# Conditioning vectors moved wholly to VectorE, a quarter of each weight's low part to GpSimd, coarse recurrence copies to ScalarE

## The chip, the cores and the metric

The kernel runs on one core of one Trainium2 chip. The metric is device time in microseconds (us) of one execution, the median of several; lower is better. The engines are named as in the profile: PE is TensorE (matmuls; PEld its weight loads), DVE is VectorE, ACT is ScalarE, POOL is GpSimd, and SP is the queue that issues the loads.

## The reference

Two layers of a decoder trunk on 256 tokens of 1024 channels in float32. A conditioning vector `c` scales, shifts and gates each layer; four token mixers run beside each other; an MLP with 4096 hidden channels follows.

```python
    for l in range(DEPTH):
        cmod = (c_act @ ada_w[l] + ada_b[l])[:, None, :]
        sh1, sc1, g1, sh2, sc2, g2 = jnp.split(cmod, 6, axis=-1)
        h = _rmsnorm(x, norm_mix_g[l]) * (1.0 + sc1) + sh1
        z = h @ w_in[l]
        ...
        ya = _conv_branch(za, conv_w[l], conv_b[l], conv_ln_g[l], conv_ln_b[l])
        yb = _sparse_attn_branch(zb, positions)
        yc = _gla_branch(zc, gla_gate_w[l], gla_gate_b[l], gla_norm_g[l])
        yd = _hgrn2_branch(zd, lower_bounds[l], hgrn_norm_g[l])
        ...
        x = x + g1 * (merged @ w_o[l])
        h = _rmsnorm(x, norm_mlp_g[l]) * (1.0 + sc2) + sh2
        x = x + g2 * (jnp.square(jax.nn.relu(h @ mlp_w1[l])) @ mlp_w2[l])
```

The six parts of `cmod` (1024 numbers each) are numbered 0 to 5 in the order of the split, so that (1, 2) is the gate `g1` of layer 1. Branches C and D are gated linear recurrences.

## The kernel before

All weights pass once through one stream of slabs of 128 x 1024 float32 (512 KB), in the order in which TensorE uses them. A slab is loaded by an SP-issued DMA into one of five `raw` places. `do_split` (L429) then makes two parts of it: ScalarE rounds it to `wh` in float32r, and VectorE subtracts, `wl = raw - wh`. TensorE multiplies three times per tile: high by high, high by low, low by high. The `raw` place is free, and the next load can start, when `wl` is there. `wh` and `wl` have five places, with four more in part of the program.

The order of instructions on each engine is fixed when the program is built: the class `Flow` (L96) emits the stream and weaves in chains of smaller work (attention, recurrences, convolution, norms) by a rough model of the engines' clocks, whose costs stand in `_Meter` (L222). On the chip each engine then works through its own list in that order, and an instruction that waits holds up what stands behind it on its engine.

Conditioning. The table `PLAN` (L60) says in which stage each part (layer, part) is worked out; `spread` (L1686, L1846) puts its items evenly between the stream's. Two methods make a part:

- On VectorE (`fill`, L623): the transposed weight comes as eight slabs, one per 128 channels, and one SCALAR_TENSOR_TENSOR per slab multiplies it by `crow` (the activated `c` on all partitions) and sums it up into a column, `raw<-raw,crow` in the rows.
- On TensorE (`half`, L662), for the three parts of `ON_PE` (L61): eight slabs too, each with two float32 matmuls of 32 output rows (`mm<-raw,cb`). After each half of a part, ScalarE copies the sums out (`adapart`), four small matmuls with `self_` add them up, and VectorE copies the column.

Recurrences (`linear`, L1283). Each of the two branches builds an attention matrix `AT` (rows: `big`) by levels `lv` 0 to 6; at each level TensorE writes blocks to PSUM and VectorE copies them where a mask is set (COPY_PREDICATED, `big<-masks,b`). GpSimd makes the seven masks in the opening (`mask_consts`, L990).

GpSimd otherwise does small work: reciprocal roots (`rstd`), gate products (`Fd`, `FE`, `sgD`, `sgC`), and in the MLP `u = r * r`.

Stages, in the profiled execution: an opening up to about 52 us (conditioning parts (0, 1) and (0, 0), and the first projection); the mixers of layer 0 up to about 275; output projection and the MLP of layer 0 up to about 505; the mixers of layer 1 up to about 725; and the rest.

```python
PLAN = {('start', 0): ((0, 1), (0, 0)), ('mixers', 0): ((0, 2), (0, 3), (0, 4)), ('mlp', 0): ((0, 5), (1, 1), (1, 0), (1, 3), (1, 4)), ('mixers', 1): ((1, 2),), ('mlp', 1): ((1, 5),)}
ON_PE = ((0, 3), (0, 4), (1, 2))
...
        A.activation(s.h, s.raw, AF.Copy)
        V.tensor_tensor(s.l, s.raw, s.h.bitcast(F32), op=OP.subtract)
        raw_free.append(fl.end)
...
                V.scalar_tensor_tensor(s.raw, s.raw, 1.0, crow, op0=OP.mult, op1=OP.mult,
                                       accum_out=self.col[:, k:k + 1])
```

Of the kernel before, what the change touches and what calls it, by code (L numbers as in the profile page):

```python
# [73 lines left out]
# pieces of the input projection: columns, and how many k tiles a slab holds  # L74
# [21 lines left out]
class Flow:  # L96
    """Emission order: a stream of weight slabs for the tensor engine, with chains of smaller work
    woven in between where a rough model of the engines says that their inputs are there."""
# [109 lines left out]
    def drain(self, ch, until=None):  # L208
        """emits a chain to its end (or until something holds), and what else can go on meanwhile"""
# [12 lines left out]
class _Meter:  # L222
# [3 lines left out]
    def __getattr__(self, name):  # L226
# [3 lines left out]
        def call(*args, **kw):  # L230
# [35 lines left out]
            else:  # L266
                dur = 150.0 + 2.1 * n if name in ("tensor_tensor", "tensor_scalar") else 40.0 + 0.8 * n
# [10 lines left out]
class _Pool:  # L278
    """a pool whose tiles are short-lived: the model knows when their places are free"""
# [15 lines left out]
class Slab:  # L295
    """A piece of a weight matrix: loaded, and split into two float32r parts when it says so."""
# [10 lines left out]
class Item:  # L307
    """A step of the tensor engine's main stream: the slabs it uses, what emits it, what comes before."""
# [8 lines left out]
def trunk_kernel(ctx, tc, x, c, cT, pos, chan, ada_w, ada_t, w_in, mlp_w1, gla_gate_w,  # L317
# [26 lines left out]
    def mm_take(n):  # L344
        """n banks for the main stream; chains that hold some go on until there are enough"""
# [4 lines left out]
    def mm_get():  # L350
        """a bank for a chain"""
# [17 lines left out]
    items = []          # in the order of the tensor engine  # L369
    slabs = []          # in the order of their first use  # L370
# [8 lines left out]
    def spread(start, fill):  # L379
        """puts the items of fill between those from start on, evenly"""  # L380
# [48 lines left out]
    def do_split(i, pool):  # L429
# [13 lines left out]
        wl = pl.tile([P, 1024], F32R, name="wl", tag="wl")  # L443
        fl.freed(wh, free)
# [4 lines left out]
        V.tensor_tensor(s.l, s.raw, s.h.bitcast(F32), op=OP.subtract)  # L449
        raw_free.append(fl.end)  # L450
# [61 lines left out]
    def kslabs(w2d, k0, nk):  # L512
        """rows k0 * 128 ... of a matrix of D columns, 128 at a time"""
# [14 lines left out]
    def tok_part(h, sl, done, t, st, i, bank=None):  # L528
        """a slab's part of h @ its columns for token tile t; done gets the finished PSUM tile"""
# [15 lines left out]
    def tok_chunk(h, sl, done, before=None, only=None):  # L545
        """h @ the columns of sl, tokens on partitions"""
# [14 lines left out]
    def chan_chunk(h, sl, done, before=None, keep=False):  # L561
        """the same with the columns on partitions"""
# [42 lines left out]
    crow = consts.tile([P, D], F32, name="crow")  # L605
    ccol = consts.tile([P, KD], F32, name="ccol")
# [1379 lines left out]
```

## Time and profile before

| what | value |
|---|---|
| median of 3 runs | 941.81 us (940.19 to 946.4) |
| profiled execution, span from first to last instruction | 943.6 us |
| PE busy | 897.3 us, 95% |
| DVE busy | 713.9 us, 76% |
| ACT busy | 478.9 us, 51% |
| POOL busy | 110.4 us, 12% |
| DMA | 196.96 MB, mean 209 GB/s |

The profiled execution has no time of its own beside the span; its span lies inside the range of the three runs. Busy time is the union of an engine's instructions. Matmuls overlap in the records, so what a matmul costs is read from the distance between starts, not from its duration. All of the kernel's own operations have one line, L273, the helper that records them, so that groups are told apart by tiles. PE's granted clock is 1.00 in nearly all slices.

### The profile page before, as it was taken

What the parts mean: (1) busy time and instruction counts of PE and PEld (TensorE: products, weight loads), DVE (VectorE), ACT (ScalarE), POOL (GpSimd) and SP (SyncE); (2) the same over time, 40 slices, a digit from 0 to 9 for tenths busy, and PEclk for the clock granted to TensorE, in tenths of its full rate; (3) what the DMA queues carried; (4) which work ended last, traced back from release to release, by engine and by line L of the source; (5) the groups of instructions that cost most, each with busy time, mean ns of one, the idle gap of its engine ahead of it and who ended that gap; (6) DMA issues with size and microseconds to landing.
All of it is one profiled execution on the core that took longest, in us unless ns stands there. A gap on an engine that the chain in (4) does not pass through costs nothing. (4 is left out here: it accounts for less than half of the span.)

```text
span 943.6 us, 14391 instructions
## 1 busy us (share of the span) xinstructions
PE 897.3 (95%) x5320; PEld 753.0 (80%) x5320; DVE 713.9 (76%) x1204; ACT 478.9 (51%) x787; POOL 110.4 (12%) x158
## 2 busy tenths in 40 slices
PE   1699999999999999999999999999999999999996
PEld 1699766767778899998978887777777889999995
DVE  7989788787767878888776988887876784555553
ACT  6474754324454544444575567333455564544451
POOL 6800010101000001111110001021000001111110
PEclk9899999999999999999999999999999999999998
DMA  8878545465644598999954554445655456666641
GB/s 315 307 253 284 188 152 179 163 194 179 230 144 158 194 312 322 316 316 315 323 192 174 168 180 155 137 151 158 223 166 172 153 183 221 225 210 216 219 158 46
DMA packets 55558, 196.96 MB, mean 209 GB/s; under 512 B 6432, under 2 KB 6848, under 8 KB 55488
## 3 DMA queue, kind: packets, MB, share of 16 engines
q1 hardware_dynamic: 55488, 196.04, 61.8%
q8 instruction: 42, 0.69, 0.3%
q14 instruction: 28, 0.23, 0.1%
HBM read 194.97 MB, written 1.05 MB: 208 GB/s over the span
## 5 line engine op out<-in xcount | busy, mean ns | idle before, releaser
L273 DVE TENSOR_TENSOR wl<-raw,wh 128x1024 fp32r<-128x1024 f32 (+1 forms) x276 | 329.3, 1219 | 64.7 <-ACT wh L273 63.5
L273 ACT ACTIVATE wh<-raw 128x1024 fp32r<-128x1024 f32 (+1 forms) x276 | 277.6, 1040 | 129.9 <-DMA raw<-in_mlp_w 73.5
L273 PE MATMUL mm<-wh,hTh 128*128 128x512 f32 (+1 forms) x384 | 155.0, 404 | 8.5 <-ACT wh L273 5.1
L273 PE MATMUL mm<-wl,hTh 128*128 128x512 f32 (+1 forms) x384 | 148.1, 386 | 5.5 <-DVE wl L273 5.4
L273 PE MATMUL mm<-wh,hTl 128*128 128x512 f32 (+1 forms) x384 | 147.7, 385 | 0.0
L273 PE MATMUL mm<-h2h,wl 128*128 128x256 f32 x416 | 117.2, 282 | 0.0
L273 PE MATMUL mm<-h2l,wh 128*128 128x256 f32 x416 | 117.2, 282 | 0.0
L273 PE MATMUL mm<-h2h,wh 128*128 128x256 f32 x416 | 117.1, 282 | 0.0
L273 PEld LDWEIGHTS mm<-wh,hTh 128*128 128x128 f32 x384 | 73.2, 191 | 37.2 <-issue 11.9
L273 PE MATMUL acc<-wh,uH 128*128 128x512 f32 x256 | 101.7, 397 | 0.0
L273 PE MATMUL acc<-wl,uH 128*128 128x512 f32 x256 | 101.2, 395 | 0.5 <-DVE wl L273 0.5
L273 PE MATMUL acc<-wh,uL 128*128 128x512 f32 x256 | 101.1, 395 | 0.1
L273 DVE SCALAR_TENSOR_TENSOR raw<-raw,crow 128x1024 f32<-128x1024 f32 x72 | 90.8, 1269 | 3.0 <-DMA raw<-in_ada_t 2.7
L273 PEld LDWEIGHTS mm<-wl,hTh 128*128 128x128 f32 x384 | 73.4, 191 | 17.0 <-DVE wl L273 6.6
L273 PEld LDWEIGHTS mm<-wh,hTl 128*128 128x128 f32 x384 | 73.3, 191 | 13.8 <-DVE hTl L273 0.3
L273 PEld LDWEIGHTS mm<-h2h,wh 128*128 128x128 f32 x416 | 78.3, 188 | 1.0
L273 PEld LDWEIGHTS mm<-h2l,wh 128*128 128x128 f32 x416 | 78.3, 188 | 1.1
L273 PEld LDWEIGHTS mm<-h2h,wl 128*128 128x128 f32 x416 | 78.3, 188 | 0.1
L273 PEld LDWEIGHTS acc<-wh,uL 128*128 128x128 f32 x256 | 48.2, 188 | 11.5 <-DVE uL L273 0.5
L273 PEld LDWEIGHTS acc<-wl,uH 128*128 128x128 f32 x256 | 48.2, 188 | 11.0 <-DVE wl L273 1.1
L273 PEld LDWEIGHTS acc<-wh,uH 128*128 128x128 f32 x256 | 48.2, 188 | 9.7
L273 DVE SCALAR_TENSOR_TENSOR ca<-U,chp,ca 128x256 f32<-128x256 f32 x120 | 53.3, 493 | 0.0
(532 smaller groups left out, 1452.7 us busy)
## 6 DMA issues: line engine op xcount, KB each, us to landing
raw<-in_mlp_w SPq DMA_DIRECT2D x128, 512.0 KB, 5.1
raw<-in_w_in SPq DMA_DIRECT2D x100, 512.0 KB, 4.2
raw<-in_ada_t SPq DMA_DIRECT2D x72, 512.0 KB, 5.5
raw<-in_ada_w SPq DMA_DIRECT2D x24, 512.0 KB, 4.2
raw<-in_w_branch_out SPq DMA_DIRECT2D x16, 512.0 KB, 4.2
raw<-in_w_o SPq DMA_DIRECT2D x16, 512.0 KB, 4.2
raw<-in_w_in SPq DMA_DIRECT2D x16, 362.0 KB, 4.3
x<-in_x SPq DMA_DIRECT2D x2, 512.0 KB, 7.6
```

The lines of the kernel that those rows point to most:

```text
L273: return fn(*args, **kw)
```

## The change

The three parts that TensorE worked out go to VectorE, and with them `ON_PE`, `half`, `ccol`, `cb`, `self_` and the second layout of the weights. `PLAN` is dealt anew: the mixers of layer 0 keep their three parts (now 24 VectorE slabs where 8 were), the MLP of layer 0 has four parts instead of five (32 slabs instead of 40), and the mixers of layer 1 have (1, 3) and (1, 4) on VectorE (16 slabs) where they had (1, 2) on TensorE. The number of slabs loaded, 96, stays. In `do_split` VectorE makes the first three quarters of `wl`, GpSimd the last quarter, and the `raw` place is free when both are done. Levels 4 to 6 of the recurrences are copied by ScalarE in pieces instead of VectorE under a mask, so that GpSimd makes four masks. `_Meter`'s cost of GpSimd's elementwise work rises from 2.1 to 3.0 ns per element, which the order of emission follows.

```diff
-PLAN = {('start', 0): ((0, 1), (0, 0)), ('mixers', 0): ((0, 2), (0, 3), (0, 4)), ('mlp', 0): ((0, 5), (1, 1), (1, 0), (1, 3), (1, 4)), ('mixers', 1): ((1, 2),), ('mlp', 1): ((1, 5),)}
-ON_PE = ((0, 3), (0, 4), (1, 2))
-ON_DVE = tuple((l, p) for l in range(2) for p in range(6) if (l, p) not in ON_PE)
+PLAN = {('start', 0): ((0, 1), (0, 0)), ('mixers', 0): ((0, 2), (0, 3), (0, 4)),
+        ('mlp', 0): ((0, 5), (1, 1), (1, 0), (1, 2)), ('mixers', 1): ((1, 3), (1, 4)), ('mlp', 1): ((1, 5),)}
...
-                dur = 150.0 + 2.1 * n if name in ("tensor_tensor", "tensor_scalar") else 40.0 + 0.8 * n
+                dur = 150.0 + 3.0 * n if name in ("tensor_tensor", "tensor_scalar") else 40.0 + 0.8 * n
...
+        n = 1
+        for d in s.shape[1:]:
+            n *= d
+        cut = n * 3 // 4
...
         A.activation(s.h, s.raw, AF.Copy)
-        V.tensor_tensor(s.l, s.raw, s.h.bitcast(F32), op=OP.subtract)
-        raw_free.append(fl.end)
+        raw = s.raw.rearrange("p a b -> p (a b)") if len(s.shape) == 3 else s.raw
+        V.tensor_tensor(wl[:, :cut], raw[:, :cut], wh[:, :cut].bitcast(F32), op=OP.subtract)
+        end = fl.end
+        G.tensor_tensor(wl[:, cut:n], raw[:, cut:n], wh[:, cut:n].bitcast(F32), op=OP.subtract)
+        raw_free.append(max(end, fl.end))
...
-            if (self.l, self.part) in ON_PE:
-                return [it for c_ in range(2) for it in self.half(c_)]
...
-        def half(self, c_):
...
-                        T.matmul(st["acc"][32 * j:32 * j + 32, :], cb[:, k, :], sl[i].raw[:, a, :],
-                                 start=k < 4, stop=k >= 4)
...
-        for lv in range(7):
+        for lv in range(4):
...
-                V.copy_predicated(ov, mk[:, None, :, :].to_broadcast([P, 2, 4 * nb, m]), dv)
+                if lv < 4:
...
+                    V.copy_predicated(ov, mk[:, None, :, :].to_broadcast([P, 2, 4 * nb, m]), dv)
+                else:
+
+                    ov = AT.rearrange("p (a e) (b two i) -> p a e b two i", a=2, two=2, i=m)
+                    dv = ps[:, :, 0:256].rearrange("p a (e b i) -> p a e b i", e=4, i=m)
+                    yield "act"
+                    for b_ in range(nb):
+                        ks = slice(2 * m * b_, 2 * m * b_ + m)
+                        A.activation(ov[ks, :, :, b_, 1, :], dv[ks, :, :, b_, :], AF.Copy)
```

What it does to the order of instructions, at three places. First TensorE, in the mixers of layer 0, where the recurrence of branch D (`Qd,Kd`) and the attention (`PT,Z`) run between the products of the input projection. Before:

```order
L273 MATMUL b_1333<-PT,Z 64x256 x2
L273 MATMUL mm<-wh,hTh 128x512
L273 MATMUL mm<-wl,hTh 128x512
L273 MATMUL mm<-wh,hTl 128x512
...
L273 MATMUL mm<-raw,cb 32x512 x2
...
L273 MATMUL b_1393<-Qd,Kd 128x64 x8
```

Now, at the same attention product:

```order
L272 MATMUL b_1327<-PT,Z 64x256 x2
L272 MATMUL b_1381<-Qd,Kd 128x64 x8
L272 MATMUL mm<-wh,hTh 128x512
L272 MATMUL mm<-wl,hTh 128x512
L272 MATMUL mm<-wh,hTl 128x512
```

The pairs `mm<-raw,cb` are gone from here and from the 23 other places where one stood; the products of the stream follow one another directly.

Second VectorE, in the second half of the mixers of layer 0, around the norm of branch D's output (`ms`, `Fd<-b...,rstd`) and the convolution's taps (`ca`). Before:

```order
L273 TENSOR_TENSOR wl<-raw,wh 128x1024
L273 SCALAR_TENSOR_TENSOR ca<-U,chp,ca 128x256 x2
L273 TENSOR_REDUCE ms<-Fd 128x8
L273 TENSOR_SCALAR ms<-ms 128x8
...
L273 TENSOR_TENSOR wl<-raw,wh 128x1024
L273 TENSOR_TENSOR Fd<-b_1762,rstd 128x256
L273 SCALAR_TENSOR_TENSOR ca<-U,chp,ca 128x256 x2
L273 TENSOR_TENSOR Fd<-b_1762,rstd 128x256
```

Now:

```order
L272 SCALAR_TENSOR_TENSOR raw,col<-raw,crow 128x1024
L272 TENSOR_TENSOR col<-col,chp 128x8
L272 TENSOR_TENSOR wl<-raw,wh 128x768
L272 TENSOR_REDUCE ms<-Fd 128x8
L272 TENSOR_SCALAR ms<-ms 128x8
...
L272 TENSOR_TENSOR wl<-raw,wh 128x768
L272 TENSOR_TENSOR Fd<-b_1787,rstd 128x256
L272 SCALAR_TENSOR_TENSOR ca<-U,chp,ca 128x256 x4
L272 TENSOR_TENSOR wl<-raw,wh 128x768
L272 TENSOR_TENSOR Fd<-b_1787,rstd 128x256
```

A conditioning slab (`raw,col<-raw,crow`) now stands before about every second weight slab, `wl` has 768 columns, and more taps of the convolution come late: the last ten stand in one run just ahead of branch A's norm.

Third GpSimd, from the opening into the mixers of layer 0, with the masks (`mks`, `masks`). Before, the last mask and what follows it:

```order
L273 AFFINE_SELECT mks<-mks 128x256 x2
L273 CAST masks<-mks 128x256
L273 MEMSET U 128x2x30
L273 TENSOR_TENSOR sgD<-sgD,ngd 128x256 x2
L273 TENSOR_TENSOR sgC<-sgC,ngc 128x256 x2
```

Now:

```order
L272 AFFINE_SELECT mks<-mks 128x256 x2
L272 CAST masks<-mks 128x256
L272 TENSOR_TENSOR wl<-raw,wh 128x181 x8
L272 TENSOR_TENSOR wl<-raw,wh 128x256 x4
L272 MEMSET U 128x2x30
L272 TENSOR_TENSOR wl<-raw,wh 128x256 x11
L272 TENSOR_TENSOR sgD<-sgD,ngd 128x256 x2
```

The low parts of the first eight weight slabs stand behind the last of the four masks, and from there on low parts fill GpSimd's list between its old work.

## Rows read from the trace of the kernel before

**Rows 1.** The page's busy times: engine, us (share of span), instructions.

```profile
PE 897.3 (95%) x5320; PEld 753.0 (80%) x5320; DVE 713.9 (76%) x1204; ACT 478.9 (51%) x787; POOL 110.4 (12%) x158
```

**Rows 2.** Who TensorE waited for: us in total, times, longest.

```profile
PE mm L273 <- DVE wl L273: 6.9, 5, 2.6
```

**Rows 3.** Three stretches: length, busy us (instructions) of PE, PEld, DVE, ACT, POOL, PEclk, DMA.

```profile
52.00:275.00 223.00, 220.24 (x1257) 168.04 (x1256) 181.28 (x348) 111.39 (x177) 14.61 (x14) 0.99 0.59 194
505.00:725.00 220.00, 217.73 (x1268) 174.99 (x1268) 175.43 (x337) 111.53 (x178) 15.26 (x14) 1.00 0.52 162
303.00:472.00 169.00, 167.55 (x1101) 152.44 (x1100) 137.25 (x194) 82.00 (x125) 22.05 (x23) 1.00 0.86 299
```

**Rows 4.** Timeline of TensorE, 121.8 to 143.5: start us, us, what.

```profile
121.83 0.39 PE L273 MATMUL mm<-wl,hTh 128*128 128x512 f32 x1
122.05 0.40 PE L273 MATMUL mm<-wh,hTl 128*128 128x512 f32 x1
122.38 1.05 PE L273 MATMUL mm<-raw,cb 128*32 128x512 f32 x4
123.36 0.50 PE L273 MATMUL mm<-wh,hTh 128*128 128x512 f32 x1
123.70 0.39 PE L273 MATMUL mm<-wl,hTh 128*128 128x512 f32 x1
...
142.45 0.95 PE L273 MATMUL mm<-self__100,adapart 128*128 128x1 f32 x8
143.26 0.48 PE L273 MATMUL mm<-wh,hTh 128*128 128x512 f32 x1
```

**Rows 5.** Groups of VectorE from 52 to 275: xcount | busy us, mean ns | idle before.

```profile
L273 DVE TENSOR_TENSOR wl<-raw,wh 128x1024 fp32r<-128x1024 f32 x59 | 72.3, 1246 | 12.3 <-ACT wh L273 12.2
...
L273 DVE SCALAR_TENSOR_TENSOR raw<-raw,crow 128x1024 f32<-128x1024 f32 x8 | 9.7, 1214 | 0.0
...
L273 DVE TENSOR_TENSOR gate<-gate 128x512 f32<-128x512 f32 x10 | 6.9, 692 | 0.3
```

**Rows 6.** Groups of VectorE from 505 to 725, the same columns.

```profile
L273 DVE TENSOR_TENSOR wl<-raw,wh 128x1024 fp32r<-128x1024 f32 x62 | 75.2, 1225 | 23.6 <-ACT wh L273 23.6
```

**Rows 7.** VectorE's masked copies: duration ns min/median/max, first and last start.

```profile
L273 DVE COPY_PREDICATED big<-masks,b x28: 684/728/1321, 120.9 to 642.2; 128x512 f32<-128x512 uint8 x28
```

**Rows 8.** Timeline of VectorE and GpSimd in the mixers, 175 to 180.6.

```profile
175.09 1.21 DVE L273 TENSOR_TENSOR wl<-raw,wh 128x1024 fp32r<-128x1024 f32 x1
...
178.39 0.98 POOL L273 TENSOR_TENSOR Fd<-Fd,sgD 128x256 f32<-128x256 f32 x1 [0.76 <-DVE Fd L273]
...
178.71 1.75 DVE L273 TENSOR_TENSOR wl<-raw,wh 128x1024 fp32r<-128x1024 f32 x1
```

**Rows 9.** Timeline of VectorE and GpSimd in the first MLP, 403 to 405.8.

```profile
403.15 1.23 DVE L273 TENSOR_TENSOR wl<-raw,wh 128x1024 fp32r<-128x1024 f32 x1 [1.12 <-ACT wh L273]
...
403.46 1.38 POOL L273 TENSOR_TENSOR u__3923<-r__3922 128x256 f32<-128x256 f32 x1 [9.74 <-ACT r__3922 L273]
...
404.81 0.61 POOL L273 TENSOR_TENSOR u__3929<-r__3928 128x256 f32<-128x256 f32 x1
...
404.88 0.82 DVE L273 TENSOR_TENSOR uL<-u__3923,uH 128x256 fp32r<-128x256 f32 x1 [0.51 <-POOL u__3923 L273]
```

**Rows 10.** The same in the second MLP, VectorE alone at its work, 797.9 to 799.2.

```profile
798.64 0.42 DVE L273 TENSOR_TENSOR uL<-u__7850,uH 128x256 fp32r<-128x256 f32 x1 [4.57 <-POOL u__7850 L273]
```

**Rows 11.** Timeline of GpSimd in the opening: the end of the fourth mask.

```profile
33.14 0.40 POOL L273 CAST masks<-mks 128x256 uint8<-128x256 f32 x1
```

**Rows 12.** Timeline of TensorE in the opening: first low product, last step's first product.

```profile
24.30 0.67 PE L273 MATMUL mm<-wl,hTh 128*128 128x362 f32 x1 [1.31 <-DVE wl L273]
...
48.53 0.43 PE L273 MATMUL mm<-wh,hTh 128*128 128x362 f32 x1 [1.53 <-ACT hTh L273]
```

More of the change, by code (lines that the diff above doesn't have):

```diff
@@ L605, in trunk_kernel @@
     crow = consts.tile([P, D], F32, name="crow")
-    ccol = consts.tile([P, KD], F32, name="ccol")
-    cb = consts.tile([P, KD, 32], F32, name="cb")
-    self_ = consts.tile([P, P], F32, name="self_")
-    G.memset(self_, 0.0)
-    for j in range(4):
-        G.memset(self_[32 * j:32 * j + 1, :], 1.0)
     class Vec:
@@ L623, in fill @@
         def fill(self, first=False):
-            if (self.l, self.part) in ON_PE:
-                return [it for c_ in range(2) for it in self.half(c_)]
             res = []
             for k in range(KD):
-                s = Slab(ada_t[ON_DVE.index((self.l, self.part)), k], [P, D], split=False)
+                s = Slab(ada_t[self.l, self.part, k], [P, D], split=False)
                 s.first = first
@@ L660, in use @@
             return f
-        def half(self, c_):
-            i_ = ON_PE.index((self.l, self.part))
-            sl = [Slab(ada_w[i_, c_, i], [P, 2, 512], split=False) for i in range(4)]
-            st = {}
-            def column():
-                yield "act"
-                src = work.tile([P, 512], F32, name="adapart", tag="t512", bufs=5)
-                A.activation(src, st["acc"], AF.Copy)
-                mm_free(st["acc"])
-                yield
-                ps = yield from mm_get()
-                for j in range(4):
-                    T.matmul(ps[:, j:j + 1], src[:, j * P:(j + 1) * P], self_[:, 0:1], start=True, stop=True)
-                yield "dve"
-                if c_ == 0:
-                    self.col = rows.tile([P, KD], F32, name="col", tag="col", bufs=8)
-                V.tensor_copy(self.col[:, 4 * c_:4 * c_ + 4], ps[:, 0:4])
-                mm_free(ps)
-                if c_ == 1:
-                    self.finish(0, KD)
-            def emit(i):
-                def f():
-                    if i == 0:
-                        st["acc"] = mm_take(1)[0]
-                    for a in range(2):
-                        k = 2 * i + a
-                        j = k % 4
-                        T.matmul(st["acc"][32 * j:32 * j + 32, :], cb[:, k, :], sl[i].raw[:, a, :],
-                                 start=k < 4, stop=k >= 4)
-                    if i == 3:
-                        fl.spawn("ada", column())
-                return f
-            return [Item(emit(i), [sl[i]], None, 600.0) for i in range(4)]
         def to_row(self):
@@ L1354, in linear @@
                 yield "dve"
-                ov = AT.rearrange("p (a e) (b two i) -> p a (e b) two i", a=2, two=2, i=m)[:, :, :, 1, :]
-                dv = ps[:, :, 0:256].rearrange("p a (k i) -> p a k i", i=m)
-                mk = cst["masks"][:, lv, :].rearrange("p (k i) -> p k i", i=m)
                 ns = w // (2 * m)
@@ L1376, in linear @@
                     seg = sn[:, :ns]
[L1377 removed]
+                if lv < 4:
+                    ov = AT.rearrange("p (a e) (b two i) -> p a (e b) two i", a=2, two=2, i=m)[:, :, :, 1, :]
+                    dv = ps[:, :, 0:256].rearrange("p a (k i) -> p a k i", i=m)
+                    mk = cst["masks"][:, lv, :].rearrange("p (k i) -> p k i", i=m)
+                    V.copy_predicated(ov, mk[:, None, :, :].to_broadcast([P, 2, 4 * nb, m]), dv)
[6 more added lines that the diff above has]
+                        A.activation(ov[ks, :, :, b_, 1, :], dv[ks, :, :, b_, :], AF.Copy)
                 self.free(ps)
@@ L1950, in _layout @@
          eight(a['norm_mix_g']), eight(a['norm_mlp_g'])], axis=2))
-    w_pe, w_dve = ([a['ada_w'][l][:, p * D:(p + 1) * D] for l, p in which] for which in (ON_PE, ON_DVE))
-    arrays['in_ada_w'] = np.stack([w.reshape(4, 2, P, 2, 512).transpose(3, 0, 2, 1, 4).reshape(2, 4, P, D)
-                                   for w in w_pe])
-    arrays['in_ada_t'] = np.stack([w.reshape(D, KD, P).transpose(1, 2, 0) for w in w_dve])
+    arrays['in_ada_t'] = np.ascontiguousarray(
+        a['ada_w'].reshape(depth, D, 6, KD, P).transpose(0, 2, 3, 4, 1))
     pieces = []
```

10 lines of the change are left out of this document (2 added, 8 removed).

## The prediction

> **What bounds the kernel now.** I read the busy times first, then who waited, then the two stages that the change works on, then single stretches of the timeline. TensorE is busy for 897.3 of 943.6 us, VectorE for 713.9, GpSimd for 110.4 [rows 1]. Busy alone could mislead, since matmuls overlap in the records; the list of TensorE's waits settles it: its longest sum of waits for weights is 6.9 us in five places [rows 2]. So the time is TensorE's own list of matmuls, and an edit gains what it takes out of that list unless something new is late. What could be late is read by stage [rows 3]. The mixers of layer 0 (52 to 275) have TensorE at 220.2 of 223 and VectorE already at 181.3, the mixers of layer 1 (505 to 725) 217.7 and 175.4 of 220. In the first MLP VectorE has 137.3 of 169. In every stage GpSimd has hardly anything, ScalarE about half.
>
> **What leaves TensorE.** One conditioning item is two float32 matmuls, four records [rows 4]: the run starts at 122.38 and the next product at 123.36, 0.98 us. Around it the stream slows: the product ahead takes 0.33 us to the next start (122.05 to 122.38) and the one behind 0.34 (123.36 to 123.70), where 0.22 is usual (121.83 to 122.05). That is 0.11 and 0.12 more, so 1.21 us an item. A run of `self_` matmuls takes 0.81 (142.45 to 143.26); with the same 0.12 behind it, an estimate from the other place, 0.93. Layer 0 has two parts, 16 items and 4 such runs: 16 x 1.21 + 4 x 0.93 = 23.1 us. Layer 1 has one part, half of that: 11.5. In all 34.6 us, all of it on the path, which puts TensorE's floor at 223 - 23.1 = 199.9 in the mixers of layer 0 and 220 - 11.5 = 208.5 in layer 1.
>
> **What VectorE gets and gives.** A conditioning slab costs it 1.21 us [rows 5]; layer 0's mixers get 16 more and layer 1's 16 more, +19.4 each. The first MLP loses 8, -9.7. A quarter of a low part: 512 columns cost 0.69 and 1024 cost 1.23 [rows 5], so 256 columns save 0.265. With 59 and 62 slabs [rows 5, 6] that is -15.6 and -16.4. The masked copies of the three coarse levels cost 0.73 each at the median [rows 7]; two branches, so 6 in a layer, -4.4. Without any side effect VectorE's work becomes 181.3 + 19.4 - 15.6 - 4.4 = 180.7 in layer 0 and 175.4 + 19.4 - 16.4 - 4.4 = 174.0 in layer 1: below TensorE's floors, but at 90% of the first.
>
> **What the shared work costs.** GpSimd's 256 columns take 0.61 us when nothing else runs, and 1.38 when they start 0.31 after a VectorE subtraction: they then end 0.46 after it [rows 9]. The other way round, a subtraction that starts 0.32 after GpSimd takes 1.75 instead of 1.21 [rows 8], and one that takes 0.42 alone takes 0.82 beside GpSimd [rows 9, 10]. So two-input work of the two engines hardly overlaps: each quarter costs VectorE between nothing (it was idle, or read PSUM) and 0.54 us. That is more than the 0.265 that it takes off. I take 0.45 for three quarters of the slabs, since the low parts, conditioning slabs, convolution taps and recurrence products that fill most of VectorE's list have two inputs of that kind: 59 x 0.45 x 0.75 = 19.9 in layer 0, 62 x 0.45 x 0.75 = 20.9 in layer 1. VectorE then has 200.6 and 194.9; the ends are 180.7 to 212.6 (59 x 0.54) and 174.0 to 207.5. The Trainium skill (SBUF — State Buffer, Who interferes with whom) says that a VectorE instruction with two SBUF inputs and a GpSimd instruction that reads SBUF exclude each other, and that whichever comes first keeps the port for its whole length. By that rule the trace agrees on the direction, but what VectorE lost here is 0.40 to 0.54 and not the whole 0.61; with 0.61 for every slab layer 0 would stand at 216.7.
>
> **What becomes of the mixers.** In layer 0 the two engines then have equal work, 199.9 and 200.6, in lists that wait for one another. VectorE sat idle for 41.7 us of the stage, 12.2 of it waiting for `wh`, a wait that goes when it lags [rows 3, 5]; of the rest, waits on products that TensorE has not reached, I keep 11 us, between nothing and the whole 41.7. The stage takes about 211.6, 11.4 less than before, and not 23.1 less. In layer 1 VectorE with the same 11 has 206, just under TensorE's 208.5; 2 us of friction give 210.5, 9.5 less.
>
> **Costs put at nothing or little.** A low part is ready some 0.2 us later (three quarters in 0.96, then 0.46, against 1.23), hidden by the slabs that are split ahead of their use; where that cover is gone it is 0.2 a slab. The `raw` place is held as much longer and the next load starts later; in the first MLP, where DMA is busiest at 0.86, eight loads fewer outweigh that. VectorE there goes, with its 64 slabs, from 137.3 to 137.3 - 9.7 - 64 x 0.265 + 64 x 0.45 = 139.4, under TensorE's 167.6. GpSimd's own list grows in the two mixer stages by at most 121 x 1.38 = 167 us of 443. ScalarE's copies are seven short ones a branch and layer, far under its idle half. In the opening the first low parts stand behind the fourth mask, which ends at 33.5 [rows 11], while TensorE took the first at 24.30 [rows 12]. It could lose 9.2 us there, but its last step starts at 48.53 on a late input of its own [rows 12], and it has idle time to catch up: I take +1, between -2 (VectorE is rid of three masks beside it) and +9. The norms between the stages wait for GpSimd's roots, now behind low parts: +1, between 0 and +4.
>
> **The sum.** -11.4 - 9.5 + 1 + 1 = -18.9 us on a span of 943.6. The span lies within the range of the three runs, 1.8 above their median, so I take the same from the median: 941.8 - 18.9 = 922.9, rounded to 923.
>
> **Rivals.**
> - *TensorE's floor is reached.* GpSimd's quarters fall where VectorE is idle or reads PSUM, and the mixers stay bound by TensorE. For it: VectorE's 180.7 and 174.0 without exclusion, and 41.7 us of idle time. Against: at 90% its list is hardly ever empty. All 34.6 go, less 1 for the opening: about 908.
> - *The gain is given back in the mixers.* Every quarter costs 0.54: 212.6 and 207.5 of work, with 11 idle 223.6 and 218.5, that is +0.6 and -1.5. With the +2 of opening and norms about 943, no change. For it: in rows 8 and 9 no two-input instruction escapes. The Trainium skill (Perfetto Trace Analysis, Optimizing Scalar/DVE Operations) warns that moving work between these two engines may not help because they share a read port; rows 8 and 9 bear that out for one instruction, no row for a stage.
> - *Slower: VectorE is late and keeps its idle time.* If each quarter costs GpSimd's full 0.61 and half the idle time stays because the order was fixed for other durations, layer 0 takes 216.7 + 20.9 = 237.6 (+14.6) and layer 1 174.0 + 37.8 + 22.3 = 234.1 (+14.1): with the +2 about 973. At 0.54 a quarter it decides from 10.4 us of kept idle time in layer 0 on. Against: those waits are for TensorE, and a late VectorE finds them over. For it: the last ten taps of the convolution now stand in one run ahead of branch A's norm, which TensorE needs.
>
> **Chances.** A change of 1% (9.4 us) is about what a measurement of this kernel can tell from none. Forecast (913 to 932): 0.47. TensorE's floor (905 to 913): 0.16. Given back (932 to 951): 0.23. Slower: 0.14. So faster by over 1% 0.63, within 1% 0.23, slower 0.14. The forecast's own range is 911 to 933; the range that should hold 8 times in 10 runs from the floor, 908, to the end of the case that gives the gain back, 950.
>
> **What would show it.** Right: no `mm<-raw,cb` on TensorE; `wl` on VectorE at 0.96 where it is alone and 1.4 to 1.5 where GpSimd stands in the way; GpSimd's quarters at 0.6 alone and over 1 in the mixers; conditioning slabs of layer 0's mixers near 1.2 to 1.7; the mixers of layer 0 about 212 long with VectorE busy over 90%, those of layer 1 about 211; both MLPs as long as before. Wrong: `wl` near 0.96 everywhere would mean no exclusion and a time near 908; waits of TensorE for VectorE's or GpSimd's `wl` over some 25 us in the mixers would mean no gain; a TensorE start later than some 55 us into the projections behind the opening would mean that the masks hold it up.

## The result, and the profile after

The changed kernel takes 956.28 us (median; 956.09 to 961.9) against 941.46 for the kernel before: ratio 1.016, 95% interval 1.0124 to 1.0195. It is slower by 1.6%, where 923 was forecast and the range ended at 950. The profiled execution has a span of 954.4 us, against 943.6.

The page's busy times after, as in [rows 1]:

```profile
PE 883.0 (93%) x5176; PEld 755.3 (79%) x5176; DVE 760.0 (80%) x1234; ACT 489.9 (51%) x810; POOL 435.7 (46%) x416
```

TensorE has 144 instructions fewer, the 96 of the pairs and the 48 of the `self_` runs, as the change says. VectorE has 46 us more to do and GpSimd 325 more. TensorE's busy time fell by only 14 us, although 24 items and 6 runs are gone: what stayed got slower.

The stages, cut where the products of the next stage begin, so that the two kernels can be compared (the prediction cut its stretches a few us elsewhere; lengths in us):

| stage | before | after | difference |
|---|---|---|---|
| opening, cut at 52 in both | 52.0 | 52.0 | |
| mixers, layer 0 | 227.9 | 228.6 | +0.7 |
| output product, layer 0 | 23.7 | 24.8 | +1.1 |
| first MLP | 168.7 | 169.2 | +0.5 |
| norm to layer 1 | 21.3 | 19.8 | -1.5 |
| mixers, layer 1 | 232.3 | 239.6 | +7.3 |
| output product, second MLP, end | 217.7 | 220.4 | +2.7 |

So TensorE's 34.6 us came off its list, and the two stages that should have become shorter by 11.4 and 9.5 became longer. The same three stages in the view of stretches, with the columns of [rows 3], first before and then after:

```profile
52.00:279.90 227.90, 225.14 (x1278) 171.99 (x1277) 184.83 (x351) 115.33 (x182) 14.61 (x14) 0.99 0.59 194
303.60:472.30 168.70, 167.25 (x1101) 152.27 (x1100) 136.95 (x193) 81.70 (x125) 22.05 (x23) 1.00 0.85 300
493.60:725.90 232.30, 228.43 (x1329) 184.68 (x1329) 184.82 (x354) 118.18 (x193) 15.80 (x15) 1.00 0.53 167
```

```profile
52.00:280.60 228.60, 209.05 (x1175) 169.78 (x1174) 200.83 (x373) 117.75 (x188) 85.87 (x75) 0.94 0.58 193
305.40:474.60 169.20, 167.38 (x1101) 152.65 (x1100) 139.13 (x181) 87.84 (x134) 94.16 (x88) 0.99 0.82 286
494.40:734.00 239.60, 226.39 (x1280) 186.22 (x1281) 207.42 (x382) 124.44 (x207) 92.18 (x80) 0.96 0.54 180
```

Three things are to be seen. VectorE's work, 200.8 and 207.4, is close to what the prediction's terms give on this cut (204.1 and 204.3, worked out below). But VectorE still sits idle for 27.8 us of the first stretch and 32.2 of the third, where 11 were allowed. And TensorE, which had 2.8 us without a matmul in layer 0, now has 19.6, at a mean granted clock of 0.94 where it was 0.99. Neither engine is busy throughout any more; they wait for one another. Whom TensorE waits for, the first rows (us in total, times, longest):

```profile
PE accs L272 <- ACT ynorm L272: 15.4, 2, 13.8
PE b L272 <- DVE dg L272: 7.7, 2, 5.0
PE mm L272 <- POOL wl L272: 6.1, 1, 6.1
PE mm L272 <- ACT yshA L272: 5.3, 2, 3.8
PE mm L272 <- ACT wh L272: 3.5, 3, 2.6
PE mm L272 <- DVE yslC L272: 3.0, 2, 2.1
PE b L272 <- DVE Qx L272: 2.1, 1, 2.1
```

Set against [rows 2], the waits are no longer for weights. They are for results of the branches' chains: `dg` and `Qx` of the recurrences, `yshA` and `yslC` of the norms. (The first and the third row are the opening. The 13.8 is the wait for the first input of all, 14.5 in the kernel before. The 6.1 for GpSimd's `wl` puts nothing behind: by 52 us TensorE has worked through 117 matmuls, before the change 108.) The place with the most of it in layer 0 is the norm of branch A. TensorE's timeline there after (start, duration, line, operation, count, idle time before and its releaser):

```profile
252.54 0.40 PE L272 MATMUL mm<-wh,hTl 128*128 128x512 f32 x1
254.83 1.10 PE L272 MATMUL b<-ca,onesd 128*128 128x256 f32 x4 [1.90 <-DVE ca L272]
257.38 1.20 PE L272 MATMUL b<-onesd,U 128*128 128x1 f32 x8 [1.44 <-ACT U L272]
259.60 1.23 PE L272 MATMUL b<-ident,rstd 128*128 128x128 f32 x4 [1.02 <-POOL rstd L272]
264.64 0.79 PE L272 MATMUL mm<-wh,yshA 128*128 128x512 f32 x1 [3.81 <-ACT yshA L272]
```

The same norm before:

```profile
248.07 1.13 PE L273 MATMUL b<-ca,onesd 128*128 128x256 f32 x4
...
252.69 0.95 PE L273 MATMUL b<-onesd,U 128*128 128x1 f32 x8
...
257.03 0.61 PE L273 MATMUL b<-ident,rstd 128*128 128x128 f32 x4
...
263.20 0.39 PE L273 MATMUL mm<-wh,yshA 128*128 128x512 f32 x1
```

From the first matmul of this norm to the first product of its result the chain takes 15 us before and 10 after. Before, 48 products of the stream and two short runs of the conditioning's small matmuls stand in its gaps (where the "..." are), so TensorE never waits there. After, none does: the taps of the convolution are emitted later, the norm comes when the products that stood in its gaps have been issued ahead of it, and TensorE stands still for 1.90, 1.44, 1.02 and 3.81 us, 8.2 in all. VectorE's timeline in the same place shows the run of late taps, and then idle time behind each step of the same chain:

```profile
251.05 4.03 DVE L272 SCALAR_TENSOR_TENSOR ca<-U,chp,ca 128x256 f32<-128x256 f32 x10
255.97 0.69 DVE L272 TENSOR_TENSOR ca<-ca,b 128x512 f32<-128x512 f32 x1 [0.89 <-PE b L272]
258.61 0.16 DVE L272 TENSOR_SCALAR va<-b 128x2 f32<-128x2 f32 x1 [1.95 <-PE b L272]
260.93 0.69 DVE L272 TENSOR_TENSOR ca<-ca,b 128x512 f32<-128x512 f32 x1 [2.16 <-PE b L272]
```

### The profile page after: what moved, and what is told of

Read it like the earlier page. It is cut to its first block, busy times and chain, and to the rows that moved or that the text cites. A ratio compares the mean times of both kernels' runs of the same rounds, so it can differ in the third digit from the quotient of the medians.

```text
span 954.4 us, 14800 instructions
## 1 busy us (share of the span) xinstructions
PE 883.0 (93%) x5176; PEld 755.3 (79%) x5176; DVE 760.0 (80%) x1234; ACT 489.9 (51%) x810; POOL 435.7 (46%) x416
## 5 line engine op out<-in xcount | busy, mean ns | idle before, releaser
L272 POOL TENSOR_TENSOR wl<-raw,wh 128x256 fp32r<-128x256 f32 (+1 forms) x276 | 346.5, 1269 | 357.3 <-ACT wh L272 328.9
L272 DVE TENSOR_TENSOR wl<-raw,wh 128x768 fp32r<-128x768 f32 (+1 forms) x276 | 320.7, 1184 | 42.7 <-ACT wh L272 42.3
L272 DVE SCALAR_TENSOR_TENSOR raw<-raw,crow 128x1024 f32<-128x1024 f32 x96 | 131.8, 1378 | 3.5 <-DMA raw<-in_ada_t 3.3
L272 DVE SCALAR_TENSOR_TENSOR ca<-U,chp,ca 128x256 f32<-128x256 f32 x120 | 60.7, 558 | 0.0
L272 PEld LDWEIGHTS acc<-wh,uL 128*128 128x128 f32 x256 | 48.1, 188 | 11.4
```

What stands on the lines that cost most here:

```text
L272: return fn(*args, **kw)
```

## The experiments

All are compared with runs of the kernel before on the same chip, whose medians lay between 941.5 and 943.6; behind each time in us stands its ratio to that kernel with a 95% interval. Two theories stood at the start: that the shared work of VectorE and GpSimd makes VectorE late, and that the 32 conditioning slabs that the mixers got do. A third, that the order which the planner writes is at fault, turned out to be needed.

**The quarter taken away, and put alone.** The first run gives VectorE the whole low part again:

```
-        V.tensor_tensor(wl[:, :cut], raw[:, :cut], wh[:, :cut].bitcast(F32), op=OP.subtract)
-        end = fl.end
-        G.tensor_tensor(wl[:, cut:n], raw[:, cut:n], wh[:, cut:n].bitcast(F32), op=OP.subtract)
-        raw_free.append(max(end, fl.end))
+        V.tensor_tensor(s.l, s.raw, s.h.bitcast(F32), op=OP.subtract)
+        raw_free.append(fl.end)
```

> The changed kernel with every low part made whole by VectorE again; conditioning, plan and ScalarE's copies stay as changed. Theory of the shared work (GpSimd's quarter takes more from VectorE than it spares it, and that is what makes VectorE late in the mixers): wl goes from 1.18 back to about 1.22, the other two-input instructions get shorter, VectorE's work in the mixers of layer 0 falls from 200.8 to about 196, and the time falls from 956 by 10 us or more, to 935 to 946. Theory of the conditioning (the 16 slabs more in each mixer stage make VectorE late whoever makes the low parts): VectorE has about as much to do as before the edit, TensorE's waits stay, the time stays within 6 us of 956.

Measured 992.6 us, 1.0528 [1.0509, 1.0548] of before: 36 us slower than the changed kernel, which neither theory allows. VectorE's work did fall as expected. But the planner wrote another order: in layer 0 it now sets 140 instructions of the branches' chains in one row on TensorE, without a product of the stream. That stretch in the trace:

```profile
131.00:221.00 90.00, 45.76 (x266) 37.22 (x264) 57.85 (x140) 21.23 (x49) 9.41 (x9) 0.53 0.05 19
```

For 90 us TensorE is half idle at a granted clock of 0.53 (column before the last two), and the DMA engines stand at 0.05. An edit of VectorE's work and an edit of the order cannot be told apart in such a run. The next two have the same flaw, and are to be read with it. The quarter as the only edit to the kernel before (the diff above the other way round, and the planner's 3.0 for GpSimd):

> The kernel before with GpSimd's quarter of every low part (and the planner's cost for GpSimd) as the only edit: conditioning on TensorE in three parts, copies of the recurrence on VectorE. Shared work: VectorE's work over the span goes up from 714 instead of down by 276 x 0.265 = 73, by about 276 x 0.2 = 55 or more less that 73, so it stays near 714, and TensorE waits for low parts in two pieces: 945 to 960. Conditioning: the quarter costs nothing that the path sees, 938 to 945.

Measured 979.0, 1.0386 [1.0348, 1.0424]. With ScalarE's copies as well:

> The run before it with ScalarE's copies of the three coarse levels as well, so the changed kernel without the part that moves conditioning. Against the changed kernel it tells what the conditioning did: by the theory of the conditioning it is 10 us or more faster than 956; by the theory of the shared work it is as slow, 950 to 962. Against the run with the quarter alone it tells what the copies do: I expect less than 4 us either way.

Measured 971.6, 1.0306 [1.0285, 1.0328]. The step from here to the changed kernel, which is conditioning and plan, then brings 15 us: the theory of the conditioning does not stand by this, as far as a run with another order can tell. Both runs lie above every range that I had set, and the copies made 7 us of difference where I had expected less than 4.

**The planner told the measured times.**

```
             s.use()
+            fl.clock["dve"] += 250.0
...
         raw_free.append(max(end, fl.end))
+        fl.clock["dve"] += 250.0
```

> The changed kernel, the same instructions, in another order: the planner that sets the order of emission counts 0.25 us more of VectorE's time for each low part and each conditioning slab, as the trace shows them (1.18 and 1.38 us where it reckons with 0.87 and 1.13). Theory of the order (the chains are woven in too early because the planner's durations don't hold, so TensorE meets inputs that are late): 8 us or more faster, 948 or less. Shared work and conditioning: the work is what is too much, the time stays within 6 us of 956.

Measured 989.2, 1.0491 [1.0471, 1.0512]. My reason was wrong: truer durations gave a worse order, with 154 chain instructions in a row. What I take for the reason is a rule in `weave`: a chain's step that runs on VectorE is emitted only while VectorE is reckoned at most `SLACK`, 3.0 us, ahead of TensorE, but slabs are split and conditioned up to `SPLIT_SLACK`, 7.0 us, ahead. With more slabs' work on VectorE the reckoned clock can stand past 3.0 for long, and the chains are then held until something has to have them. By this reading the changed kernel's quarter, reckoned as time saved on VectorE, was what kept its order tolerable; the planner's clock itself was not recorded. The run without the quarter was repeated with one number changed:

```
-SLACK = 3000.0
+SLACK = 5000.0
```

> The run without the quarter (992.6) with one number of the planner changed: a chain's step may be emitted when VectorE is reckoned up to 5.0 us ahead of TensorE instead of 3.0. In the order TensorE then has no stretch of more than 16 instructions of the chains without a product of the stream, where that run had one of 140 in layer 0 and one of 50 in layer 1. Theory of the order: those stretches were the loss, the time falls by 30 us or more, to 960 or less. Shared work and conditioning: VectorE's work is unchanged, so the time stays within 10 us of 992.

Measured 948.2, 1.0039 [1.0022, 1.0056]: 44 us from one number, with the same work. The theory of the order holds for this loss.

**At a fixed order.** From here on a part of the work is changed while the planner is told what it was told before, so that TensorE's and ScalarE's orders stay the same but for what is taken out. First the quarter, taken from the changed kernel:

```
-        V.tensor_tensor(wl[:, :cut], raw[:, :cut], wh[:, :cut].bitcast(F32), op=OP.subtract)
+        nc.vector.tensor_tensor(s.l, s.raw, s.h.bitcast(F32), op=OP.subtract)
+        fl.note("dve", 68.0 + 1.042 * cut, [raw[:, :cut], wh[:, :cut]], [wl[:, :cut]])
...
-        G.tensor_tensor(wl[:, cut:n], raw[:, cut:n], wh[:, cut:n].bitcast(F32), op=OP.subtract)
+        fl.note("pool", 150.0 + 3.0 * (n - cut), [raw[:, cut:n], wh[:, cut:n]], [wl[:, cut:n]])
```

Here `nc.vector` emits an instruction past the planner, and `fl.note` tells the planner of one that is not there.

> The changed kernel's order kept instruction for instruction (the planner is told the same durations), but VectorE makes each low part whole and GpSimd's quarters are gone. It parts what the quarter does on the chip from what it does to the planner's order, which the run without the quarter mixed. Theory of the shared work: VectorE loses more to GpSimd than it is spared, so the time falls below 950. Theory of the order: at a fixed order the quarter is worth little either way, 950 to 962, and the 992.6 of the run without the quarter was its order. If the quarter really spares VectorE: 962 or more.

Measured 944.2, 1.0003 [0.9987, 1.002]: the quarter costs 12 us between the two medians, or 14 when each is set against the kernel before on its own chip. That is the shared work, seen in VectorE's groups over the whole run, by form (count, busy time, mean ns, idle time before). The changed kernel:

```profile
L272 DVE TENSOR_TENSOR wl<-raw,wh 128x768 fp32r<-128x768 f32 x260 | 304.9, 1193 | 42.5 <-ACT wh L272 42.3
L272 DVE SCALAR_TENSOR_TENSOR raw<-raw,crow 128x1024 f32<-128x1024 f32 x96 | 131.8, 1378 | 3.5 <-DMA raw<-in_ada_t 3.3
L272 DVE SCALAR_TENSOR_TENSOR ca<-U,chp,ca 128x256 f32<-128x256 f32 x120 | 60.7, 558 | 0.0
```

The same order with whole low parts:

```profile
L453 DVE TENSOR_TENSOR wl<-raw,wh 128x1024 fp32r<-128x1024 f32 x260 | 311.5, 1224 | 49.9 <-ACT wh L272 49.6
L272 DVE SCALAR_TENSOR_TENSOR raw<-raw,crow 128x1024 f32<-128x1024 f32 x96 | 119.0, 1246 | 2.2 <-DMA raw<-in_ada_t 2.0
L272 DVE SCALAR_TENSOR_TENSOR ca<-U,chp,ca 128x256 f32<-128x256 f32 x120 | 54.1, 502 | 0.0
```

Three quarters of a low part take VectorE 1.19 us, the whole 1.22. What the quarter should have saved, 276 x 0.265 = 73 us, it does not save, and the slabs and taps beside it get longer: VectorE's busy time is 760.0 with the quarter and 725.9 without. The quarters cost it 73 + 34 = 107 us, 0.39 each. In the same way the quarter is put into the kernel before, at that kernel's order:

> The kernel before, its order kept, with GpSimd making the last quarter of each low part. Shared work: most of the 36 us that the quarter alone cost (979.0 against 942.9) is there again, 965 or more. Order: without the planner's new order little of it is left beyond the opening, where the first low parts stand behind all seven masks (some 8 us): 945 to 957.

Measured 963.2, 1.0202 [1.0171, 1.0233]: 20 us, between what the two theories said. Of the 36 us that the quarter alone had cost with the planner's new order (979.0 against 942.9), 20 are so the shared work and 16 the order. Up to the output product of layer 0 it loses 4.5 us, with the first low parts behind seven masks, and in the first MLP 10.3 (179.0 instead of 168.7), which the fixed order of the changed kernel did not show. There are 40 conditioning slabs in that MLP, not 32. The weights come later there: ScalarE, which rounds them, waits 85.1 us for loads instead of 68.5, and TensorE waits for `wl` in seven places instead of two. The rows with the quarter, then before (waited for: us, times, longest):

```profile
PE acc L273 <- DVE wl L455: 7.3, 7, 1.7
ACT wh L273 <- DMA raw<-in_mlp_w: 85.1, 43, 5.8
```

```profile
PE acc L273 <- DVE wl L273: 0.5, 2, 0.3
ACT wh L273 <- DMA raw<-in_mlp_w: 68.5, 43, 4.2
```

That the loads start later because the `raw` places come free later is likely, and was not shown by itself.

Then the conditioning slabs, at the changed kernel's order:

```
+                if (self.l, self.part) in PLAN["mixers", 0] + PLAN["mixers", 1]:
+                    nc.vector.scalar_tensor_tensor(s.raw[:, :32], s.raw[:, :32], 1.0, crow[:, :32], ...)
+                    fl.note("dve", 129.0 + 1.042 * D, [crow], [s.raw, self.col[:, k:k + 1]])
+                else:
...
```

> The changed kernel's order kept, but the conditioning slabs of the mixers (24 in layer 0, 16 in layer 1) are multiplied on VectorE in their first 32 columns alone; the rest of that sum is left out. About 40 x 1.3 = 52 us of VectorE's work is gone. Theory of the conditioning: the mixers come down to TensorE's own work, 925 or less in all. Theory of the order: the chains still come in the wrong places, a good part of the waits stays, 935 or more.

Measured 942.8, 0.9994 [0.9982, 1.0005]. VectorE's busy time falls by 45 us (760.0 to 714.9; 52 were expected) and 13.5 are gained, so the slabs cost something, but with VectorE's list as light as before the change and TensorE's 34.6 us shorter the time is only that of the kernel before. GpSimd's quarters are still in this run. Both edits together:

> The changed kernel's order kept, with both loads on VectorE gone: low parts whole on VectorE without GpSimd (944.2 alone) and the conditioning slabs of the mixers multiplied in 32 columns alone (942.8 alone, the rest of that sum left out). TensorE's list is 34.6 us shorter than before and VectorE has less to do than before. Theory that VectorE's work is all that went wrong: the two gains add up or more, 931 or less, toward TensorE's floor of 908. Theory that the conditioning matmuls had been filling time in which TensorE would have waited for the branches' chains anyway: the gains overlap, 934 to 942.

Measured 934.4, 0.9894 [0.9872, 0.9916], the end that I had set for the gains that overlap. The question was then whether the conditioning matmuls had been on TensorE's path at all:

```
-                        T.matmul(st["acc"][32 * j:32 * j + 32, :], cb[:, k, :], sl[i].raw[:, a, :],
-                                 start=k < 4, stop=k >= 4)
+                        if k == 0:
+                            nc.tensor.matmul(st["acc"], cb[:, 0:4, :].rearrange("p a b -> p (a b)"),
+                                             sl[i].raw[:, a, :], start=True, stop=True)
...
```

> The kernel before, its order kept, with one full-height matmul in place of every eight pairs' worth of conditioning matmuls on TensorE (the rest of that sum left out): about 7/8 of 24 x 1.21 = 25 us leave TensorE's list, VectorE and GpSimd unchanged. The prediction's first term (all of it is on the path): 941.5 - 25 = 917, at most 920. Theory of the filling: TensorE then waits for the chains instead, half or less is gained, 929 or more.

Measured 923.2, 0.9788 [0.9753, 0.9822]: 20.4 of the 25 us are gained, between the two theories and near the first. (One matmul stands for eight, which are four of the pairs of [rows 4].) At the order of before these matmuls were on the path. The two stretches of the mixers, first of this run, then of the run with both edits:

```profile
52.00:265.00 213.00, 208.64 (x1221) 170.40 (x1221) 183.86 (x351) 114.54 (x181) 15.78 (x14) 1.00 0.62 208
475.90:701.90 226.00, 221.90 (x1302) 184.46 (x1302) 184.51 (x354) 118.05 (x193) 15.81 (x15) 1.00 0.51 172
```

```profile
52.00:271.00 219.00, 208.08 (x1167) 170.27 (x1166) 172.31 (x369) 116.77 (x183) 12.49 (x13) 0.94 0.59 201
482.80:713.80 231.00, 221.49 (x1281) 183.71 (x1280) 183.16 (x380) 124.59 (x207) 13.09 (x15) 0.99 0.55 185
```

TensorE has the same work in both, a little less in the second, and VectorE no more; the second, in the changed kernel's order, is 6.0 and 5.0 us longer, with a clock of 0.94 in layer 0. That is the order, 934.4 against 923.2, as far as the two runs part it: they differ also in ScalarE's copies, which cost nothing as the only edit (942.0, below), and in eight slabs that are loaded in layer 1's mixers instead of the first MLP.

**Fillers in the waits of branch A's norm.**

```
+            def keep(ps, n):
+                for _ in range(n):
+                    nc.tensor.matmul(ps[:, 1, 256:512], dum[:, 0:P], dum, start=True, stop=True)
...
+            keep(ps, 16)
```

> The changed kernel, its order kept, with 64 matmuls of 256 columns on a constant (results unused) put into the four waits of branch A's norm in each layer: 64 x 0.118 = 7.6 us of TensorE's time where the trace has it waiting 8 us in layer 0. Theory of the clock (after these waits the granted clock is 0.50 from 257 to 271 and the products behind take 0.43 us each instead of 0.23): the clock stays up and 4 to 6 us of layer 0 come back, 950 to 953. If the clock had no part, the matmuls gain nothing or are in the way: 956 or more.

Measured 968.0, 1.0271 [1.0232, 1.031]. This is inconclusive for the clock. The fillers wrote into the chain's own pair of PSUM banks, and the steps behind them waited for them as well: the waits of 1.44 and 3.81 us stand in the trace as before, now behind the fillers, and the products behind the last wait still start 0.43 us apart. A filler with a bank of its own wasn't tried.

**Where the conditioning could go.** One part of the change alone, layer 1's part, with 8 slabs in layer 1's mixers:

```
-ON_PE = ((0, 3), (0, 4), (1, 2))
+ON_PE = ((0, 3), (0, 4))
-SLACK = 3000.0
+SLACK = 5000.0
```

> The kernel before with one part of the change alone: layer 1's part of the conditioning goes to VectorE in layer 1's mixers (8 slabs), nothing else; and the planner may run VectorE's chains 5.0 us ahead instead of 3.0, without which the new order has 120 chain instructions in one stretch. Theory of VectorE's work: it has 185 + 8 x 1.21 = 195 of 232 us there, room enough, and 11.5 us leave TensorE: 931 to 936. Theory of the filling and the order: TensorE waits for the chains instead, 938 to 946.

Measured 948.7, 1.0054 [1.0037, 1.0072]. That is above both theories. Layer 1's mixers became 1.9 us shorter (230.4), while layer 0's, whose work nobody touched, became 8.9 longer (236.8) by the other `SLACK`. Too much of it harms here, as too little did above. The next three have 4.0 (the last of them in layer 1 alone).

> The changed kernel without GpSimd's quarter, the planner 4.0 us ahead instead of 3.0, and layer 1's two parts of the conditioning moved from its mixers into the first MLP (48 slabs there, none in layer 1's mixers). In its order branch A's norm has 11.4 us of stream products behind its first matmul in layer 0 and 50 in layer 1, where the changed kernel has 0.6 and 9. Theory of the order: layer 0's mixers come down from 224 to 219 or less, layer 1's from 236 to 227 or less, the first MLP stays near 168: 922 to 935. If VectorE or the loads have no room in the first MLP (48 slabs, 20 us more for VectorE on 130 of 168, 8 MB more to load): the MLP goes to 178 or more, 938 or more.

Measured 936.4, 0.9934 [0.991, 0.9958]: the mixers at 220.1 and 224.0, near what the theory of the order said (219 and 227 at most), but the first MLP at 175.1 instead of 168. With 40 slabs in the MLP (against the run without the quarter):

```
-        ('mlp', 0): ((0, 5), (1, 1), (1, 0), (1, 2)), ('mixers', 1): ((1, 3), (1, 4)), ('mlp', 1): ((1, 5),)}
+        ('mlp', 0): ((0, 5), (1, 1), (1, 0), (1, 2), (1, 3)), ('mixers', 1): ((1, 4),), ('mlp', 1): ((1, 5),)}
...
-SLACK = 3000.0
+SLACK = 4000.0
```

> As the run before, with one of the two parts left in layer 1's mixers (40 slabs in the first MLP, as in the kernel before, and 8 in the mixers). Theory of the order: layer 0 as in the run before, layer 1's mixers at 226 to 232, 926 to 938. If VectorE's slabs are what costs, layer 1 is 5 us or more longer than with none.

Measured 934.9, 0.9913 [0.9886, 0.9939], the fastest kernel here that leaves nothing out, faster than the kernel before and the changed one. Its three stages:

```profile
52.00:272.60 220.60, 207.27 (x1165) 170.02 (x1165) 195.64 (x371) 115.76 (x183) 16.41 (x13) 0.95 0.60 200
296.50:465.00 168.50, 166.32 (x1101) 151.47 (x1101) 138.26 (x194) 83.50 (x127) 22.05 (x23) 1.00 0.86 305
484.50:712.60 228.10, 220.75 (x1281) 185.81 (x1280) 191.23 (x363) 124.44 (x207) 17.42 (x15) 0.98 0.52 170
```

In layer 0, where VectorE has the same 195 us as in the fixed-order run without the quarter, the stage is 3.4 us shorter (220.6 against 224.0), with 45 stream products inside branch A's norm instead of none. Layer 0 still stands 7.6 us above the 213.0 of the order of before.

The kernel before with layer 1's part in the first MLP:

> The kernel before, low parts, copies and layer 0 as they were; only layer 1's part of the conditioning leaves TensorE and is multiplied by VectorE in the first MLP (48 slabs there); the planner runs 4.0 us ahead in layer 1. Room in the MLP: VectorE 137 + 10 of 168, the 11.5 us of layer 1 are gained, 931 to 937. No room: the MLP gets longer by what layer 1 gains, 940 to 948.

Measured 942.6, 0.9994 [0.9977, 1.0011]. Layer 1 gains 9.2 us (223.1) and the first MLP loses 8.2:

```profile
304.00:480.90 176.90, 170.22 (x1101) 152.43 (x1100) 148.14 (x211) 83.13 (x129) 27.08 (x25) 1.00 0.87 310
```

VectorE is busy for 148 of 177 us there, the DMA engines at 0.87, and TensorE waits for `wl`. So 40 slabs fit in this MLP and 48 don't, though no engine is full. The copies alone:

> The kernel before with ScalarE's copies of the coarse levels (and four masks instead of seven) alone. TensorE is the bound and its list is the same: within 4 us of 943. If VectorE's or GpSimd's earlier end is worth something on its own, 936 or less; if ScalarE's pieces hold the chains up, 948 or more.

Measured 942.0, 0.9991 [0.9976, 1.0005]: nothing, as expected. Last, the quarter put into the run with 40 slabs, at that run's order:

> The run with 40 slabs in the first MLP (934.9), its order kept, with GpSimd making the last quarter of each low part again. Theory of the shared work: VectorE's work rises by 30 us or more over the span although a quarter of each low part is taken from it, and the time by 8 us or more, to 943 to 955. If the 12 us that the quarter cost in the changed kernel came from its late chains: less than 5 us, below 940.

Measured 951.7, 1.0076 [1.0052, 1.01]: 17 us lost, VectorE's busy time up by 25.1 (756.5 against 731.4; 30 or more were expected). 10.6 of the 17 are the first MLP with its 40 slabs; the mixers lose 1.3 and 2.7. The MLP:

```profile
298.10:477.20 179.10, 168.92 (x1100) 151.63 (x1099) 143.91 (x193) 82.25 (x126) 87.34 (x82) 1.00 0.81 283
```

The quarter costs 12, 17 and 20 us in three orders. In the first MLP, where no branch's chain runs, it costs 10.6 and 10.3 with 40 slabs and 0.8 with 32, so the loss is not one of late chains alone. In the mixers it costs 8.2 at the changed kernel's order (228.6 and 239.6 against 224.0 and 236.0) and 4.0 at this one, so that a part of it there may come from the late chains; this was not parted.

## Why the prediction was wrong, step by step

- *"What leaves TensorE", 34.6 us, all on the path:* nearly right at the order of before, 20.4 of 25 us. At the changed order, with the quarter and the mixers' conditioning slabs taken off VectorE, only 9.2 of the 34.6 are left (943.6 to 934.4).
- *VectorE's work:* right within 4 us. On the cut of the table above, the forecast is 184.8 + 19.4 - 15.6 - 4.4 + 19.9 = 204.1 for layer 0 and 184.8 + 19.4 - 16.4 - 4.4 + 20.9 = 204.3 for layer 1; the trace has 200.8 and 207.4.
- *The shared work:* right in kind and close in size: 0.45 for three quarters of the slabs is 0.34 a slab, 0.39 was measured. The Trainium skill (SBUF — State Buffer, Who interferes with whom) has the two engines exclude each other for the whole length of an instruction. The trace agrees in direction; the mean of 0.39 stays below the length of a quarter, and 135 of VectorE's 260 subtractions of 768 columns took under 1.0 us, so that many were not held up. The 0.61 that the prediction gives a quarter alone is another product's, `u = r * r` [rows 9]; the shortest quarter of 256 columns in the changed kernel took 0.72.
- *"What becomes of the mixers", 11 us of idle time kept:* this is the step that failed. VectorE kept 27.8 and 32.2, and TensorE, the larger of the two sums in layer 1, did not set that stage either: on the cut of the table its floors are 227.9 - 23.1 = 204.8 and 232.3 - 11.5 = 220.8, and the stages stand 23.8 and 18.8 above them, where the prediction allowed 11.7 and 2. I treated the idle time as slack that a fuller list uses up, and the stage as the larger of two sums. But the stage is a lattice of chains between the engines, and what hid their latencies was the order: whether stream products stand between a chain's steps (48 before and none after in branch A's norm of layer 0). The change put that order anew, and I read the new order only for what was moved, not for what no longer stood between the steps. The ten late taps in a run are told of with VectorE's order ahead of the prediction; the prediction names them in one sentence, as a point for the slower rival, and gives them no price.
- *Costs put at nothing:* the first MLP with 32 slabs (169.2 against 168.7), ScalarE's copies and the opening were right. The output products pay 1.1 each and the second MLP 1.8; I had no term for these. The quarter makes 0.8 and 0.7 of that: without it, at the same order, they stand at 24.0 and 168.4, against 23.7 and 167.3 before. That its low parts come later was not shown to be the reason.
- *The rivals:* "slower: VectorE is late and keeps its idle time" had the right mechanism, with 21 and 22 us kept idle, and 0.14. Its price of 973 was too high, since it set 0.61 for each quarter, and since it took VectorE to be the bound of the stage; here neither engine is. The sign that I had set for "no gain", waits for `wl` over some 25 us in the mixers, did not come: they are 0.7 and 0.2 us there. It looked at the weights, and the waits were for the chains.

The account, from run to run: 923.2 with most of the conditioning off TensorE at the order of before; 934.4 at the changed order with VectorE free of it (+11.2, at least: the first still holds an eighth of the matmuls); 944.2 with the mixers' conditioning slabs on VectorE (+9.8); 956.3 with the quarter (+12.1, or 14 by the ratios). Branch A's norm is the one place of the order that is shown in detail; an order with products in it again has 3.4 us less in layer 0. What the other places are worth, the 5.0 us wait for `dg` that ends at 141 first among them, was not parted.

## What to carry to other kernels

Where an order is planned from reckoned durations, an edit of the work is also an edit of the order, and the second can be worth more: 44 us here from one number of the planner. Measure the two apart by keeping the order and changing the work, and before a run look at what stands between the steps of each long chain on the bounding engine. Work of two SBUF inputs gained nothing here from being cut between VectorE and GpSimd: the part that stayed took 1.19 us in the mean, the whole 1.22.

## What the hardware did that was not expected

TensorE's granted clock fell after its waits. After those at the norm of branch A it stood at 0.50, the lower of its two levels (1.2 of 2.4 GHz), and the products there start 0.43 us apart instead of the 0.23 ahead of the norm, until 271. Two such starts from the timeline, then the view of stretches in the changed kernel (the column before the last two is the granted clock):

```profile
268.51 0.63 PE L272 MATMUL mm<-wh,yshA 128*128 128x512 f32 x1
268.94 0.63 PE L272 MATMUL mm<-wl,yshA 128*128 128x512 f32 x1
```

```profile
250.00:255.00 5.00, 3.10 (x18) 2.41 (x17) 5.00 (x12) 1.79 (x3) 0.00 (x0) 1.00 0.81 272
255.00:260.00 5.00, 2.53 (x14) 1.99 (x14) 0.93 (x3) 0.63 (x1) 0.69 (x1) 0.81 0.02 7
260.00:265.00 5.00, 1.19 (x5) 0.89 (x5) 2.59 (x5) 1.72 (x3) 0.00 (x0) 0.50 0.00 0
265.00:270.00 5.00, 4.59 (x10) 2.74 (x10) 2.48 (x4) 1.06 (x1) 1.49 (x1) 0.50 0.19 40
270.00:275.00 5.00, 5.00 (x23) 4.06 (x23) 2.93 (x5) 1.97 (x3) 0.64 (x1) 0.82 0.17 68
```

From 265 to 270 TensorE is busy for 4.59 of 5 us and gets through 10 matmuls, in the next 5 us through 23. The kernel before falls to 0.66 from 265 to 270, too, but stands at 1.00 ahead of it, from 250 to 265, and again from 270. Here, then, the exposed chain was paid for twice: while TensorE waited, and in the products that followed. How much of the 14.8 us this second part is was not shown.

GpSimd's quarters took 1.27 us each in the mean (346.5 us for 276), where the shortest of 256 columns took 0.72: both engines were slower while they shared the work.
